# Last sums of a gated feed-forward tile issued behind the next gate job's fifth product; the norms' scales spread by transposes

## The chip, the cores and the metric

The kernel runs on one core of one Trainium2 chip, in one launch. The metric is device microseconds of that core. TensorE (PE in the profile, PEld for its weight loads) multiplies; ScalarE (ACT), VectorE (DVE) and GpSimd (POOL) do the rest, and transfers are issued from the queues of SyncE (SP), ScalarE and GpSimd.

## What is computed

One inference step of a two-layer decoder on 512 prompt tokens and 32 sample tokens, 544 columns in all, with a model width of 1024. Layer 0 mixes by a gated short convolution, layer 1 by retention with four heads. After each mixer comes a feed-forward of hidden width 2816. Every block starts from an RMS norm.

```python
def rmsnorm(x, g):
    y = xf * lax.rsqrt(jnp.mean(xf * xf, axis=-1, keepdims=True) + RMS_EPS)
    return (y * g.astype(jnp.float32)).astype(x.dtype)

def swiglu(x, w_gate, w_up, w_down):
    return (jax.nn.silu(x @ w_gate) * (x @ w_up)) @ w_down

for i in range(DEPTH):
    h = rmsnorm(x, norm_mix[i])
    m = short_conv_mixer(h, ...) if i % 2 == 0 else retention_mixer(h, ...)
    x = x + m
    x = x + swiglu(rmsnorm(x, norm_ffn[i]), ffn_w_gate[i], ffn_w_up[i], ffn_w_down[i])
return rmsnorm(x, final_norm), ...
```

## The kernel before

**Layout.** Activations lie transposed: 128 features on the partitions and 544 tokens along the free dimension, as two halves of 272. Every float32 operand is split into a high and a low part (`split`, L202 on ScalarE and L203 on VectorE), and a product is three matmuls: high by high, high by low, low by high.

**Seven products.** The two projections of a feed-forward, and its down projection for most tiles, are done in blocks of 2 by 2 with seven products in place of eight (`Job`, whose matmuls are all at L386). A product has 12 matmuls with a moving operand of 272 columns in a gate or up job, and 9 in most down jobs. A job makes product 1 in a PSUM bank `a`; then come products 6 (into `a`), 5 (into a third bank `c`, from the pool `mm`), 2 (into a bank `b`) and 7 (into `a`); then, in `end`, product 3 into `c` and product 4 into `a`. `take` reads a bank after each step: the products named `u1`, `u2` and `p5` are copied to SBUF by ScalarE (L445, in `summed`), those named `c11`, `c12` and `u3` are added to the copies by VectorE (L447). Product 3 adds to `c` after `p5`, so its first matmul has to wait for the copy of `p5`.

**Order of jobs.** `run` takes the jobs in a row. For each it issues the weight work of the next job (`prepare`), products 6, 5, 2 and 7 of this job, product 1 of the next, and products 3 and 4 of this one. `weights7` does the weight work: sums of the 2 by 2 blocks on VectorE (L336 to L339), splits (L202 and L203; L315 to L317 for the mixed form) and a transfer that adds weights from DRAM to a low part (L318, issued by GpSimd).

**Hidden tiles.** Each layer has 11 pairs of hidden tiles, m = 0 to 10, each with a gate job and an up job (`gate_up`). The gate job ends with the norm's scale, the silu and the scale again (L782 to L785), the up job with products by the gate (L790 to L794). After the up job, `tail(m)` prepares the operands of the down projection: for m = 0 to 8 differences (L717, L720, L721), two splits, a copy of four blocks on ScalarE (`ht`, L722), a negative copy (`lt`, L723) and a transfer that adds the blocks to `lt` (L724, issued by GpSimd). For m = 3 and 6 the tail runs behind the down jobs of the group of three tiles before (`later`); m = 9 and 10 have a plain split. The down jobs of a group come after the next m's gate and up jobs.

**The norms.** `rms_scale` sums squares over features with matmuls that put the sums on the partitions (L272), takes the power -0.5 (GpSimd, L248) into columns of `rN`, waits a number of steps, and then spreads each column over all partitions with a float32 matmul of the column, broadcast to 128 by 128, and an identity (`spread`, L252). It runs four times: in the convolution, in both feed-forwards and before the retention. Six matmuls cover the 544 tokens, of 128, 128, 16, 112, 128 and 32 columns. The last norm does the same in `scale`, for each half of the tokens, with three matmuls of 128, 128 and 16 columns.

**Order of instructions.** The framework puts each engine's instructions in an order by dependences, a model of durations and the order in which the code issues them. That order is fixed when the program is built. Every engine works through its own in order.

Of the kernel before, what the change touches and what calls it, by code (L numbers as in the profile page):

```python
# [7 lines left out]
F32 = mybir.dt.float32  # L8
F32R = mybir.dt.float32r
AF = mybir.ActivationFunctionType  # L10
ALU = mybir.AluOpType

P = 128
D = 1024
KT = D // P
SEQ = 512
NB = 8
DS = 4
NS = NB * DS
# [4 lines left out]
HT = T // 2  # L24
# [28 lines left out]
def hybrid_decode_kernel(ctx: ExitStack, tc: tile.TileContext, a: dict, o: dict):  # L53
    nc = tc.nc
# [6 lines left out]
    def nm(s):  # L61
        uid[0] += 1
        return f"{s}_{uid[0]}"
# [3 lines left out]
    kinds, at = ["m"], [0]  # L67
# [5 lines left out]
    def psum():  # L73

        kind = kinds[0][at[0] % len(kinds[0])]
        at[0] += 1
        if kind == "s":
            return [bank(), bank()]
        return ps.tile([P, 2, 512], F32, tag="mm", name=nm("mm"), bufs=2)
# [4 lines left out]
    def half(pt, hf):  # L84
        return pt[hf] if isinstance(pt, list) else pt[:, hf, :]

    def each(fn, pt, *aps):

        if isinstance(pt, list):
            for hf in range(2):  # L90
                fn(pt[hf][:, :HT], *[ap[:, hf, :] for ap in aps])
        else:
            fn(pt[:, :, :HT], *aps)
# [5 lines left out]
    mask_p, where_p, rest = cb[:, :512], cb[:, 512:1024], cb[:, 1024:1312]  # L99
    mask_s, ident, mean_w = rest[:, :NS], rest[:, NS : NS + P], rest[:, NS + P :]  # L100
# [33 lines left out]
    rN = resid.tile([P, 6], F32, tag="rN", name="rN")  # L134
# [107 lines left out]
    def rsqrt(out, var, n, eps=None):  # L242

        if eps is None:
            nc.vector.tensor_scalar_add(out, var, EPS)
        else:
            nc.vector.tensor_add(out, var, eps)
        nc.gpsimd.tensor_tensor(out, out, expo[: out.shape[0], :n], op=ALU.pow)  # L248

    def spread(out, tt, lo, hi):  # L250

        return nc.tensor.matmul(  # L252
            out, rN[:, tt : tt + 1].to_broadcast([P, P]), ident[:, lo:hi], start=True, stop=True, skip_group_check=True
        )

    def rms_scale(sample=False, pt=None, rest=4):

        n = 6 if sample else 5  # L260
        pt = pt or psum()
        ms = half(pt, 0)[:, 496:502]
        cols = [slice(tt * P, (tt + 1) * P) for tt in range(4)] + [slice(T - P, T), slice(SEQ, T)]
        for tt in range(n):
            lhs = sqacc[:, cols[tt]]
            if tt == 5:
                lhs = sqlast[:, :P]
                nc.vector.tensor_copy(
                    lhs.rearrange("p (g c) -> p g c", c=NS),
                    sqacc[:, SEQ:].unsqueeze(1).to_broadcast([P, P // NS, NS]),  # L270
                )
            nc.tensor.matmul(ms[:, tt : tt + 1], lhs, mean_w[:, 0:1], start=True, stop=True)  # L272
            if tt < n - 1:
                yield
        rsqrt(rN[:, :n], ms[:, :n], n)
        for _ in range(rest):
            yield

        for tt, hf, at, lo, hi in (
            (0, 0, 0, 0, P), (1, 0, P, 0, P), (2, 0, 2 * P, 0, HT - 2 * P),  # L280
            (2, 1, 0, HT - 2 * P, P), (3, 1, 3 * P - HT, 0, P), (4, 1, SEQ - HT, P - NS, P),
        ):
            spread(half(pt, hf)[:, at : at + hi - lo], tt, lo, hi)
        each(lambda p, r: nc.scalar.activation(r, p, AF.Copy), pt, R)

    def drain(steps):
# [167 lines left out]
    with ExitStack() as c0:  # L454
# [65 lines left out]
        sums = {}  # L520
# [67 lines left out]

        c, b = temp("c"), temp("b")
        nc.gpsimd.memset(u[:, :, NSLOT : NSLOT + 2], 0.0)  # L590
        steps = rms_scale(rest=5)
        pts = [start()]
        for d, pt in zip((b, c), pts[0]):
            each(lambda p, di: nc.scalar.activation(di, p, AF.Copy), pt, halves(d[:, 0, :]))
# [67 lines left out]
        for i, n in enumerate(PAIRED[0]):  # L662
            if i < 2:
                wh, wl, pt = early[i]
                project(pt, wh, wl, 0, yh, yl, first=False, ks=(KT - 2, KT - 1))
            else:
                wh, wl = load_piece(a["cvout"][n], KT * P)
                pt = psum()
# [4 lines left out]
    def ffn(layer, next_gain, then=None):  # L673
        with ExitStack() as c1:
# [19 lines left out]
                s = m % KP  # L694
                return (xh[s], xh[s + KP]), (xl[s], xl[s + KP])

            turned = {}

            def seven(m):

# [8 lines left out]
            def tail(m, g, u):  # L709
                if m >= last[0]:  # L710
                    hs, ls = hidden(m)
                    for i in range(2):
                        split(hs[i], ls[i], u[:, i, :])
                    return
                b, t = [v.rearrange("p a (b c) -> p (a b) c", b=2) for v in (u, g)]
                (h1, h2, ht), (l1, l2, lt) = seven(m)
                nc.vector.tensor_sub(t[:, 0:2, :], b[:, 1::2, :], b[:, 0:2, :])  # L717
                split(h1, l1, b[:, 0:1, :])
                split(h2, l2, b[:, 2:4, :])
                nc.vector.tensor_sub(t[:, 2, :], b[:, 3, :], t[:, 0, :])  # L720
                nc.vector.tensor_sub(t[:, 3, :], b[:, 2, :], t[:, 2, :])  # L721
                nc.scalar.activation(ht, t, AF.Copy)  # L722
                nc.scalar.activation(lt, ht.bitcast(F32), AF.Copy, scale=-1.0)  # L723
                nc.gpsimd.dma_start(lt, t, accum_op=ALU.add)  # L724
                turned[m] = [
                    {1: p[0][:, 0, :], 2: p[1][:, 0, :], 3: p[1][:, 1, :],
                     5: p[2][:, 0, :], 7: p[2][:, 1, :], 6: p[2][:, 2, :], 4: p[2][:, 3, :]}
                    for p in ((h1, h2, ht), (l1, l2, lt))
                ]
# [40 lines left out]
            def gate_up(m):  # L770
                made = {}

                def tile2(tag):
                    if tag not in made:
                        made[tag] = tp.tile([P, 2, T], F32, tag="gu", name=nm(tag))
                    return made[tag]

                def gate(what, src):
                    g = tile2("g")
                    r = R.rearrange("p a b -> p (a b)").unsqueeze(1).to_broadcast([P, 2, T])  # L780
                    if what == "c21":
                        nc.scalar.activation(g[:, 1, :HT], src, AF.Copy)  # L782
                        nc.vector.tensor_mul(g, g, r)
                        nc.scalar.activation(g, g, AF.Silu)
                        nc.vector.tensor_mul(g, g, r)  # L785

                def up(what, src):
                    g, u = tile2("g"), tile2("u")
                    if what == "u3":
                        nc.vector.tensor_mul(u[:, 1, HT:], u[:, 1, HT:], g[:, 1, HT:])  # L790
                    elif what == "c12":
                        nc.vector.tensor_mul(u[:, 0, :], u[:, 0, :], g[:, 0, :])
                    elif what == "c21":
                        nc.vector.tensor_mul(u[:, 1, :HT], src, g[:, 1, :HT])  # L794
                        if m and m % GROUP == 0:

                            later[m] = lambda: tail(m, g, u)
                        else:
                            tail(m, g, u)

                return [
                    Job(
                        [a["ffgu"][layer, 2 * j + q] for j in (m, m + HJ)],
                        lambda k, which: [t[k][:, OPERAND[which], :] for t in (oh, ol)], sw,
                        summed(lambda tag="gu"[q]: tile2(tag), (gate, up)[q]),
                        (lambda: psum()[:, 0, :]) if m else None,
                    )
                    for q in range(2)
                ]
# [67 lines left out]
            steps = rms_scale(rest=9)  # L877
# [10 lines left out]
    def final(ms, acts, group_weights, fp, tp):  # L888
# [4 lines left out]
        sums = {}  # L893
# [21 lines left out]
        def scale(hf):  # L915
            pt = bank()
            mq = pt[:, 496:499]

            of = (sqacc, sqlast)[: hf + 1]
            for t in of:  # L920
                for i, at in enumerate((0, P, HT - P)):
                    cols = slice(hf * HT + at, hf * HT + at + P)
                    last_sum[hf] = nc.tensor.matmul(
                        mq[:, i : i + 1], t[:, cols], mean_w[:, 0:1], start=t is of[0] and (hf == 0 or i == 0),
                        stop=t is of[-1], skip_group_check=True,
                    )
                if t is not of[-1]:
                    yield
            with tc.issue_after(first_product[0].ins) if hf else ExitStack():
                nc.vector.tensor_scalar_add(rN[:, :3], mq, EPS)  # L930
            powers[hf] = nc.gpsimd.tensor_tensor(rN[:, :3], rN[:, :3], expo[:, :3], op=ALU.pow)
            yield
            for i, (lo, hi) in enumerate(((0, P), (0, P), (3 * P - HT, P))):
                last_spread[0] = spread(pt[:, i * P : i * P + hi - lo], i, lo, hi)
            sums[hf] = pt[:, :HT]

        def copied(hf):
# [16 lines left out]
        last_sum, last_spread, powers, first_product, last_store = {}, [None], {}, [None], [None]  # L954
# [18 lines left out]
        rest = scale(1)  # L973
# [796 lines left out]
```

## Time and profile before

| what | value |
|---|---|
| three runs: median (lowest to highest) | 1404.88 us (1404.77 to 1405.04) |
| the profiled execution's own time | 1405.36 us |
| its span, from first to last instruction | 1403.6 us |
| TensorE, busy of the span | 99% |
| VectorE, ScalarE, GpSimd, busy of the span | 81%, 59%, 16% |
| granted TensorE clock, mean | 0.999 |

The profile is of one execution. A line such as `L386 PE MATMUL sm<-oh,wh` is the source line, the engine, the operation, and the tile that is written and those that are read, without buffer numbers. Matmuls overlap: one takes 0.29 us from start to end, while the next starts after 0.12 us. So the distance from start to start tells what a matmul costs, and a busy TensorE may still hold short waits. A float32 matmul that isn't a split product is recorded as two.

### The profile page before, as it was taken

Reading aid. Unit: us, or ns where it says so; the run is one execution under the profiler, and the core shown is the slowest. Engines: PE = TensorE matmul, PEld = TensorE weight load, DVE = VectorE, ACT = ScalarE, POOL = GpSimd, SP = SyncE. Lnnn points to the kernel's source line nnn. Section 1 sums busy time; section 2 is a strip of 40 time slices with the busy share of each in tenths; the row PEclk is TensorE's granted clock in tenths of the full one; section 3 lists DMA queues with packets and bytes.
Section 4 is the critical chain, followed back from the end, with each engine's and each line's share of the span. In section 5 each row is a group of like instructions: output and inputs, shape, how many; then the busy total and the mean of one; then the engine's idle time right before and its main releaser. Section 6 shows DMA issues by size and latency. Waiting matters only on the chain.

```text
span 1403.6 us, 26578 instructions
## 1 busy us (share of the span) xinstructions
PE 1390.2 (99%) x10454; PEld 1317.3 (94%) x10454; DVE 1132.1 (81%) x1923; ACT 822.9 (59%) x1286; POOL 219.4 (16%) x255
## 2 busy tenths in 40 slices
PE   9999999999999999999999999999999999999997
PEld 8999999999999999999967877877899999999997
DVE  6987889898989878676867576586799898989884
ACT  7666567667677657666632313224387767677654
POOL 0111011212221213111200000000111212121212
PEclk9999999999999999999999999999999999999999
DMA  6476346777676754677667355465766777777742
GB/s 206 119 169 166 108 106 159 168 173 183 143 188 151 168 120 134 185 199 201 212 212 240 121 209 184 144 235 181 211 143 153 169 176 172 154 184 153 165 106 87
DMA packets 99295, 233.69 MB, mean 166 GB/s; under 512 B 9793, under 2 KB 33489, under 8 KB 98785
## 3 DMA queue, kind: packets, MB, share of 16 engines
q1 hardware_dynamic: 68032, 167.47, 38.4%
q0 software_dynamic: 28688, 56.61, 23.5%
q10 hardware_dynamic: 2448, 7.91, 1.5%
q8 instruction: 82, 1.34, 0.4%
q14 instruction: 45, 0.36, 0.1%
HBM read 191.84 MB, written 28.42 MB: 157 GB/s over the span
## 4 chain that ended last, share of the span: by engine, by line
PE 93%; DVE 2%; issue 2%; DMA 2%; POOL 0%; ACT 0%; SPq 0%; DVEq 0%; POOLq 0%; ACTq 0%
PE sm L386 43%; PE mm L386 16%; PE mm L187 14%; PE sm L187 4%; PE sm L1262 2%; PE sm L1264 2%; PE sm L1263 2%; PE sm L175 2%; PE sm L177 1%; PE sm L176 1%; PE sm L1483 1%; DVE S L1506 1%; PE mm L1270 1%; DMA wl<-in_rtout_dram 1%; PE mm L1422 0%
## 5 line engine op out<-in xcount | busy, mean ns | idle before, releaser
L386 PE MATMUL sm<-oh,wh 128*128 128x272 f32 x856 | 247.8, 289 | 0.5 <-DVE b L447 0.5
L386 PE MATMUL sm<-ol,wh 128*128 128x272 f32 x856 | 246.1, 288 | 0.0
L386 PE MATMUL sm<-oh,wl 128*128 128x272 f32 x856 | 246.1, 287 | 0.0
L202 ACT ACTIVATE h<-w 128x1024 fp32r<-128x1024 f32 (+3 forms) x170 | 136.5, 804 | 106.3 <-PE mm L386 92.9
L203 DVE TENSOR_TENSOR l<-w,h 128x1024 fp32r<-128x1024 f32 (+3 forms) x170 | 153.6, 904 | 28.1 <-ACT h L202 25.3
L315 ACT ACTIVATE wh<-w 128x1024 fp32r<-128x1024 f32 (+1 forms) x134 | 133.7, 998 | 56.7 <-PE sm L386 48.5
L386 PEld LDWEIGHTS sm<-oh,wh 128*128 128x128 f32 x856 | 161.3, 188 | 2.0 <-DVE b L447 0.9
L386 PEld LDWEIGHTS sm<-oh,wl 128*128 128x128 f32 x856 | 161.1, 188 | 0.0
L386 PEld LDWEIGHTS sm<-ol,wh 128*128 128x128 f32 x856 | 160.8, 188 | 0.1
L386 PE MATMUL sm<-parts,wh 128*128 128x272 f32 x736 | 142.5, 288 | 0.0
L202 ACT ACTIVATE wh<-w 128x1024 fp32r<-128x1024 f32 (+3 forms) x76 | 68.0, 898 | 120.3 <-PE mm L187 62.1
L318 POOL DMA_DIRECT2D wl<-in_ffgu_dram x87 | 81.7, 939 | 328.2 <-ACT wl L317 94.2
L386 PE MATMUL mm<-oh,h 128*128 128x272 f32 x396 | 115.5, 292 | 0.0
L386 PEld LDWEIGHTS sm<-parts,wh 128*128 128x128 f32 x736 | 115.5, 188 | 0.0
L386 PE MATMUL mm<-oh,l 128*128 128x272 f32 x396 | 113.5, 287 | 0.0
L386 PE MATMUL mm<-ol,h 128*128 128x272 f32 x396 | 113.3, 286 | 0.0
L316 DVE TENSOR_TENSOR wl<-w,wh 128x512 fp32r<-128x512 f32 (+1 forms) x134 | 87.2, 651 | 26.4 <-ACT wh L315 26.2
L386 PE MATMUL sm<-parts,wl 128*128 128x272 f32 x368 | 106.2, 289 | 0.3 <-DMA wl<-in_rtqk_dram 0.2
L317 ACT ACTIVATE wl<-wh 128x512 fp32r<-128x512 f32 (+1 forms) x173 | 102.8, 594 | 2.0
L203 DVE TENSOR_TENSOR wl<-w,wh 128x1024 fp32r<-128x1024 f32 (+3 forms) x76 | 79.8, 1055 | 13.1 <-ACT wh L202 12.4
L187 PE MATMUL mm<-parts,wh 128*128 128x272 f32 x488 | 82.4, 290 | 1.4 <-ACT wh L202 1.4
L386 PE MATMUL sm<-oh,h 128*128 128x272 f32 x284 | 82.2, 289 | 0.0
(377 smaller groups left out, 3837.7 us busy)
## 6 DMA issues: line engine op xcount, KB each, us to landing
w<-in_ffgu_dram SPq DMA_DIRECT2D x66, 512.0 KB
wl<-in_ffgu_dram POOLq DMA_DIRECT2D x87, 256.0 KB, 5.2
S<-in_rets_dram SPq DMA_DIRECT2D x16, 1024.0 KB
out_rets_dram<-S SPq DMA_DIRECT2D x16, 1024.0 KB
w<-in_ffdn_dram SPq DMA_DIRECT2D x36, 384.0 KB
cb<-in_ffgu_dram SPq DMA_DIRECT2D x22, 512.0 KB
w<-in_cvin_dram SPq DMA_DIRECT2D x21, 512.0 KB
wl<-in_ffdn_dram POOLq DMA_DIRECT2D x48, 192.0 KB, 4.8
```

The lines of the kernel that those rows point to most:

```text
L175: nc.tensor.matmul(out, lh, rh, start=start, stop=False, skip_group_check=True)
L187: last_product[0] = nc.tensor.matmul(half(pt, hf)[:, :HT], w[:, c], act[k][:, hf * HT : (hf + 1) * HT], start=(first and k == ks[0] and i ...
L202: h = nc.scalar.activation(dh, src, AF.Copy)
L203: last_low[0] = nc.vector.tensor_sub(dl, src, dh.bitcast(F32))
L315: nc.scalar.activation(wh, w, AF.Copy)
L316: last_mixed[0] = nc.vector.tensor_sub(wl[:, :n], w[:, :n], wh[:, :n].bitcast(F32))
L317: nc.scalar.activation(wl[:, n:], wh[:, n:].bitcast(F32), AF.Copy, scale=-1.0)
L318: nc.gpsimd.dma_start(wl[:, n:], src[:, 1, :] if len(src.shape) == 3 else src[:, n:], accum_op=ALU.add)
L386: last = nc.tensor.matmul(out, w[:, c], b, start=(first and j == 0 and i == 0), stop=(j == len(self.ks) - 1 and i == 2), skip_group_check= ...
L1262: nc.tensor.matmul(out, xh[kt][:, ts_], wh[:, cw], start=(kt == 0), stop=False)
L1263: nc.tensor.matmul(out, xh[kt][:, ts_], wl[:, cw], start=False, stop=False)
L1264: last = nc.tensor.matmul(out, xl[kt][:, ts_], wh[:, cw], start=False, stop=(kt == KT - 1))
```

## The change

1. `spread` makes a transpose of the broadcast column, in place of a matmul with the identity, when it has 128 columns. `rms_scale` takes pieces of 128 columns where it can: the third piece of the first half and the last piece of the second are widened, and one of 112 columns stays a matmul. In the convolution's norm nothing changes (`turned=False`). The last norm's third pieces are widened too.
2. In `tail`, the copy `ht`, the negative copy `lt` and the transfer are put on a list. The next gate job issues them when its `p5` has been copied.

```diff
+    def spread(out, tt, lo=0, hi=P, turned=True):
+
+        column = rN[:, tt : tt + 1].to_broadcast([P, P])
+        if turned and hi - lo == P:
+            return nc.tensor.transpose(out, column, ident)
+        return nc.tensor.matmul(out, column, ident[:, lo:hi], start=True, stop=True, skip_group_check=True)
...
-        for tt, hf, at, lo, hi in (
-            (0, 0, 0, 0, P), (1, 0, P, 0, P), (2, 0, 2 * P, 0, HT - 2 * P),
-            (2, 1, 0, HT - 2 * P, P), (3, 1, 3 * P - HT, 0, P), (4, 1, SEQ - HT, P - NS, P),
+        whole = (0, P)
+        for tt, hf, at, (lo, hi) in (
+            (0, 0, 0, whole), (1, 0, P, whole), (2, 0, 2 * P, whole if turned else (0, HT - 2 * P)),
+            (2, 1, 0, (HT - 2 * P, P)), (3, 1, 3 * P - HT, whole),
+            (4, 1, HT - P, whole) if turned else (4, 1, SEQ - HT, (P - NS, P)),
         ):
-            spread(half(pt, hf)[:, at : at + hi - lo], tt, lo, hi)
+            spread(half(pt, hf)[:, at : at + hi - lo], tt, lo, hi, turned)
...
-        steps = rms_scale(rest=5)
+        steps = rms_scale(rest=5, turned=False)
...
-                nc.scalar.activation(ht, t, AF.Copy)
-                nc.scalar.activation(lt, ht.bitcast(F32), AF.Copy, scale=-1.0)
-                nc.gpsimd.dma_start(lt, t, accum_op=ALU.add)
+
+                def sums():
+                    nc.scalar.activation(ht, t, AF.Copy)
+                    nc.scalar.activation(lt, ht.bitcast(F32), AF.Copy, scale=-1.0)
+                    nc.gpsimd.dma_start(lt, t, accum_op=ALU.add)
+
+                waiting.append(sums)
...
-                    if what == "c21":
+                    if what == "p5":
+                        while waiting:
+                            waiting.pop(0)()
+                    elif what == "c21":
...
-            for i, (lo, hi) in enumerate(((0, P), (0, P), (3 * P - HT, P))):
-                last_spread[0] = spread(pt[:, i * P : i * P + hi - lo], i, lo, hi)
+            for i, at in enumerate((0, P, HT - P)):
+                last_spread[0] = spread(pt[:, at : at + P], i)
```

In the built program the two versions differ on each engine as follows. On ScalarE, at 14 places (m = 0, 1, 2, 4, 5, 7, 8 of both layers) the copy of `p5` stands ahead of `ht`; before it stood behind `ht`, a weight copy (L315), `lt` and a second weight copy (L317). For m = 3 and 6 the order is the same as before. At 8 of the 14 (m = 0, 1, 4, 7) the silu (L784) has changed places with a weight split (L202) later in the gate job. On VectorE the additions of `c11` and `u3` (L447) each move ahead of weight work, and at the same 8 places the second scaling of the gate (L785) moves ahead of a weight split (L203); at the first down job of a group some sums change places with additions to `x`. On TensorE, three matmuls of the up job's product 5 stood ahead of the gate job's product 3 at each of the 14 places and now stand behind its product 4; beside that only the spreads differ. The orders on SyncE and on GpSimd are the same.

More of the change, by code (lines that the diff above doesn't have):

```diff
@@ L248, in rsqrt, with rms_scale @@
         nc.gpsimd.tensor_tensor(out, out, expo[: out.shape[0], :n], op=ALU.pow)
[L250 to L256, printed above, removed]
+    def spread(out, tt, lo=0, hi=P, turned=True):
[3 more added lines that the diff above has]
+        return nc.tensor.matmul(out, column, ident[:, lo:hi], start=True, stop=True, skip_group_check=True)
+    def rms_scale(sample=False, pt=None, rest=4, turned=True):
         n = 6 if sample else 5
@@ L695, in hidden @@
                 return (xh[s], xh[s + KP]), (xl[s], xl[s + KP])
-            turned = {}
+            turned, waiting = {}, []
             def seven(m):
```

## The prediction

> **What bounds the kernel.** I read the page first, then TensorE's busy time by stretches, then the order of time around the moved copy.
>
> ```profile
> PE 1390.2 (99%) x10454; PEld 1317.3 (94%) x10454; DVE 1132.1 (81%) x1923; ACT 822.9 (59%) x1286; POOL 219.4 (16%) x255
> PE 93%; DVE 2%; issue 2%; DMA 2%; POOL 0%; ACT 0%; SPq 0%; DVEq 0%; POOLq 0%; ACTq 0%
> ```
>
> TensorE is busy for 99% of the span and holds 93% of the chain that ended last. So what counts is what TensorE has to do and where it is held up. Matmuls overlap, so a short hold-up hides in "busy". It shows in the weight loads (PEld), which run without a gap when nothing holds them:
>
> ```profile
> core 0: us, PE busy (x) PEld busy (x) DVE busy (x) ACT busy (x) POOL busy (x), PEclk, DMA share, GB/s
> 208.00:470.00 262.00, 262.00 (x2090) 261.10 (x2088) 234.57 (x411) 184.13 (x291) 54.77 (x63) 1.00 0.73 165
> 1051.00:1312.00 261.00, 261.00 (x2081) 260.10 (x2081) 233.75 (x410) 184.07 (x291) 54.77 (x63) 1.00 0.74 166
> 269.00:332.00 63.00, 63.00 (x507) 63.00 (x506) 54.99 (x101) 42.06 (x67) 13.69 (x16) 1.00 0.76 175
> ```
>
> The first two stretches hold most of the gate, up and down jobs of the two feed-forwards, with the seven places of each where a moved tail stood; in each the loads miss 0.90 us. The third lies between two of the tails that the change moves, and there they miss nothing. It also gives the price of a matmul: 63 us / 506 = 0.1245 us, call it 0.125. Seven tails of a layer are moved, so 0.90 / 7 = 0.13 us of missing loads would fall to each. The place itself:
>
> ```profile
> 225.87 0.29 PE L386 MATMUL mm<-ol,h 128*128 128x272 f32 x1
> 226.00 0.29 PE L386 MATMUL mm<-oh,l 128*128 128x272 f32 x1
> 226.19 0.40 PE L386 MATMUL mm<-oh,h 128*128 128x272 f32 x1
> 226.42 0.29 PE L386 MATMUL mm<-ol,h 128*128 128x272 f32 x1
> 226.19 0.19 PEld L386 LDWEIGHTS mm<-oh,h 128*128 128x128 f32 x1
> 221.12 0.29 PE L386 MATMUL mm<-oh,l 128*128 128x272 f32 x1
> 221.32 1.06 ACT L202 ACTIVATE h<-w 128x1024 fp32r<-128x1024 f32 x1 [0.26 <-PE mm L386]
> 222.29 1.10 ACT L722 ACTIVATE parts<-g 128x1088 fp32r<-128x1088 f32 x1
> 223.29 1.04 ACT L315 ACTIVATE wh<-w 128x1024 fp32r<-128x1024 f32 x1
> 224.24 1.10 ACT L723 ACTIVATE parts<-parts 128x1088 fp32r<-128x1088 f32 x1
> 225.24 0.61 ACT L317 ACTIVATE wl<-wh 128x512 fp32r<-128x512 f32 x1
> 225.76 0.38 ACT L445 ACTIVATE g<-mm 128x272 f32<-128x272 f32 x1
> ```
>
> Product 5 of the gate job is finished when its last matmul ends, at 221.12 + 0.29 = 221.41. Its copy (L445, `g<-mm`) stands behind `ht` (L722), a weight copy, `lt` (L723) and another weight copy, and ends at 225.76 + 0.38 = 226.14. The first matmul of product 3, at 226.19, comes just after that. Its load starts together with it, where a load usually leads, and it lasts 0.40 us in place of 0.29. From 226.00 to 226.42 two steps take 0.42 us where 2 x 0.125 = 0.25 is the price: 0.17 us lost, of which 0.13 are the missing loads. So ScalarE, idle 41% of the span, holds up TensorE here by its order alone.
>
> **Part 1, the tails.** The copy moves ahead of `ht`, behind the weight split that ends at 221.32 + 1.06 = 222.38. Product 5 is ready by then, so ScalarE doesn't wait for it, and the copy ends near 222.7: 3.4 us sooner, and 3.3 us before product 3, which starts at about 226.0 once the three matmuls ahead of it are behind product 4. The wait goes. Gain: 14 x 0.17 = 2.4 us, between 0 (something else takes its place) and 14 x 0.2 = 2.8 (the rows' rounding).
>
> What is queued behind the copy is 0.38 us later: `ht`, the weight copy, `lt`, the second weight copy, which ends at 226.2. The copies after that keep their times, since `p5` was ahead of them before too. `lt`'s transfer is issued 0.4 us later, on GpSimd, and its order against the weight transfers (L318) is kept, so these are at most 0.4 us later too. The first moved tail whose `lt` is read soon is that of m = 2:
>
> ```profile
> L724 POOL DMA_DIRECT2D f<-g x6: 865/865/893, 267.9 to 1301.1; - x6
> DMA to landing us min/median/max: 6.0/6.8/9.5
> L386 PEld LDWEIGHTS sm<-f,h x48: 187/188/192, 282.0 to 1338.9; 128*128 128x128 f32 x48
> ```
>
> Issued at 267.9 and landed 9.5 us later at the latest, 277.4, or 277.8 when moved. The down jobs read these blocks first at 282.0: 4 us are left. It costs nothing. SyncE's order is the same; its loads wait for weight buffers that come free at most some tenths later.
>
> **Part 2, the spreads.** Four transposes of the retention stand beside the spreads of the second feed-forward's norm:
>
> ```profile
> 1049.24 1.42 PE L252 MATMUL mm<-cb,rN 128*128 128x128 f32 x12
> 1050.50 0.37 PE L386 MATMUL sm<-oh,wh 128*128 128x272 f32 x1
> 741.52 0.60 PE L1422 MATMUL mm<-cb,yn 128*128 128x128 f32 x4
> 741.88 0.48 PE L175 MATMUL sm<-mid,qkhl 128*128 128x512 f32 x1
> 742.20 0.39 PE L176 MATMUL sm<-mid,qkhl 128*128 128x512 f32 x1
> L1422 PE MATMUL mm<-cb,yn x64: 270/273/329, 741.5 to 1003.2; 128*128 128x128 f32 x64
> ```
>
> The six matmuls are recorded as 12: each goes through twice. From 1049.24 to the next matmul are 1.26 us, and that one lasts 0.37 in place of 0.29, so 0.08 more is theirs: 1.34 us, or 0.112 a pass, whatever its width (the 16 and 32 columns are in this mean). The four transposes are recorded once each. To the next matmul are 0.36 us, and that one lasts 0.48 in place of 0.39: 0.45, or 0.11 each. Five transposes and one matmul of two passes make 5 x 0.11 + 2 x 0.112 = 0.77. A norm gains 1.34 - 0.77 = 0.57 us, and three norms (both feed-forwards, retention) gain 1.7. All three stand in a stream of matmuls, so a shorter spread is time of the path. No row shows a transpose of a broadcast column, but the spread reads the same broadcast as its weights now; the bounds are 0 and 1.7.
>
> Weighed against that: the Trainium skill, "TensorE: Matmul & The Clock Gate", section "Part 4: PE-mode transpose", says that a 128 x 128 transpose takes about 275 ns in a kernel and doesn't count as activity for the clock gate. Its figure agrees with the 0.273 us of the row as the time from start to end; as a price in a stream it doesn't, for four would make 1.1 us and the row has 0.60 from the first start to the last end. By it as a price a norm would lose 0.25 us. What it says of the clock no row here shows for so short a run of transposes.
>
> In the last norm three matmuls of two passes become three transposes, 0.67 to 0.33 us, twice:
>
> ```profile
> 1391.64 0.81 PE L923 MATMUL sm<-cb,sqacc 128*128 128x1 f32 x6
> 1391.73 0.43 ACT L234 ACTIVATE sqlast<-x 128x272 f32<-128x272 f32 x1 [0.18 <-DVE x L902]
> 1392.32 0.81 PE L923 MATMUL sm<-cb,sqlast 128*128 128x1 f32 x6
> 1394.38 0.84 PE L252 MATMUL sm<-cb,rN 128*128 128x128 f32 x6
> 1394.30 2.91 POOL L947 TENSOR_TENSOR ya<-ya,R 128x272 f32<-128x272 f32 x4
> ```
>
> After the first spread TensorE sums squares; the last sums (1392.32) need `sqlast`, ready at 1392.16, so at most 0.16 us is to be had. Behind the second spread, a copy and VectorE's products come 0.25 sooner, but GpSimd's four products end at 1397.21 either way and hold ScalarE's last stores. Between 0 and 0.4; I take 0.1.
>
> **Sum.** 2.4 + 1.7 + 0.1 = 4.2 us. The profiled execution took 1405.36 us, 0.48 above the median of the runs: 1401.2 in its own time, 1400.7 as a median.
>
> **Rivals.**
>
> *The wait stays, with another name.* Product 3 or 4 waits for something that was hidden behind the copy. Against it: VectorE's addition of `u3`, which product 4 needs, itself waited for that copy and comes sooner now; stretches without a moved tail miss no loads. For it: VectorE is 81% busy. Only part 2 is left: 1404.9 - 1.8 = 1403.1. Chance 0.10.
>
> *A transpose holds TensorE from start to end.* 5 x 0.273 + 0.22 = 1.59 against 1.34: three norms lose 0.75, the last one some 0.1. 1404.9 - 2.4 + 0.85 = 1403.3. This is also what the skill's figure as a price would make. Against it stands the row of four in 0.60 us. Chance 0.04.
>
> *Transfers take back what layer 0 gains.* Then of the 4.2 the half of the first feed-forward and the retention's norm go, 1.2 + 2 x 0.57 = 2.3: 1403.0. For it: the DMA share of 0.73 in the first stretch. Against it: DMA has 2% of the chain. Chance 0.08.
>
> *Slower: a weight split comes too late.* At 8 of the places (m = 0, 1, 4, 7) the silu (L784) moves ahead of a split of weights (L202), and the second scaling (L785) ahead of its low part (L203).
>
> ```profile
> 231.08 1.28 DVE L783 TENSOR_TENSOR g<-g,R 128x1088 f32<-128x1088 f32 x1
> 232.01 1.06 ACT L202 ACTIVATE h<-w 128x1024 fp32r<-128x1024 f32 x1 [0.49 <-PE mm L386]
> 232.98 1.10 ACT L784 ACTIVATE g<-g 128x1088 f32<-128x1088 f32 x1
> 233.10 1.23 DVE L203 TENSOR_TENSOR l<-w,h 128x1024 fp32r<-128x1024 f32 x1 [0.74 <-ACT h L202]
> 234.25 1.29 DVE L785 TENSOR_TENSOR g<-g,R 128x1088 f32<-128x1088 f32 x1
> 239.42 0.29 PE L386 MATMUL sm<-oh,h 128*128 128x272 f32 x1
> ```
>
> The silu then waits for L783 until 232.36 and ends at 233.46, L785 ends at 234.75, and the low part, ready at 234.33 before, is ready at 234.75 + 1.23 = 235.98, 1.65 us later. Its first reader is at 239.42, so 3.4 us are left. If they were not there and TensorE waited out 1 us at each of the 8 places, the time would be 1400.7 + 8 = 1408.7; it becomes slower from 0.5 us each. Chance 0.06.
>
> **How the numbers follow.** The forecast, 1400.7, has the other 0.72. Its own range, from the bounds of the tails and of the last norm, is 1400.0 to 1402.0. The range for 8 in 10 takes in most of the three rivals near 1403 and half a microsecond below: 1399.5 to 1403.3. About 0.2% (2.8 us) is what can be told from no change, so faster means below 1402.1. Faster: the forecast and a share of the middle rivals that come out smaller, 0.75. Same: 0.18. Slower: 0.07.
>
> **What would show it.** Right: in the stretches of the two feed-forwards the weight loads miss next to nothing; the `mm` matmul after the copy lasts 0.29 us; L722 follows the copy (L445); each norm's spread has seven records in about 0.7 us; `h` and `l` of the swapped places are ready at least 2 us ahead of TensorE. Wrong: loads still missing 0.1 us or more per moved tail, a transpose every 0.27 us, or new waits of TensorE on L203 or L318.

## The result, and the profile after

The changed kernel took 1399.64 us as a median of 7 runs (1399.59 to 1401.45), the kernel before 1404.88 (7 runs, 1404.07 to 1405.40): a ratio of 0.9964, with a 95% interval of 0.9955 to 0.9973. That is 5.2 us, where 4.2 had been forecast. The profiled execution has a span of 1397.8 us against 1403.6.

The page of the kernel after, its first part and the shares of the chain of waits:

```profile
PE 1385.4 (99%) x10433; PEld 1314.1 (94%) x10433; DVE 1131.6 (81%) x1923; ACT 824.0 (59%) x1286; POOL 219.3 (16%) x255
PE 92%; DVE 4%; DMA 1%; issue 1%; ACT 1%; POOL 0%; SPq 0%; DVEq 0%; POOLq 0%; ACTq 0%
```

TensorE bounds the kernel as before. It runs 21 records fewer: three norms save five each (12 to 7), the last one twice three. The same stretches of the two feed-forwards as before, each engine's busy time in them (the lines have moved by 3 to 10 in the code):

```profile
207.00:469.00 262.00, 262.00 (x2100) 262.00 (x2100) 236.27 (x416) 184.93 (x293) 54.78 (x63) 1.00 0.74 167
1046.00:1307.00 261.00, 261.00 (x2094) 261.00 (x2093) 235.45 (x414) 184.87 (x291) 54.76 (x63) 1.00 0.74 167
```

The weight loads (third time of a row) miss nothing, where each stretch had missed 0.90 us. The first moved tail, by ScalarE's and TensorE's order of time:

```profile
220.71 0.38 ACT L448 ACTIVATE g<-mm 128x272 f32<-128x272 f32 x1
220.99 1.10 ACT L727 ACTIVATE parts<-g 128x1088 fp32r<-128x1088 f32 x1
221.99 1.05 ACT L318 ACTIVATE wh<-w 128x1024 fp32r<-128x1024 f32 x1
222.95 1.10 ACT L728 ACTIVATE parts<-parts 128x1088 fp32r<-128x1088 f32 x1
223.94 0.61 ACT L320 ACTIVATE wl<-wh 128x512 fp32r<-128x512 f32 x1
...
224.05 0.28 PE L389 MATMUL sm<-oh,wl 128*128 128x272 f32 x1
224.17 0.29 PE L389 MATMUL mm<-oh,h 128*128 128x272 f32 x1
...
225.66 0.29 PE L389 MATMUL sm<-oh,wh 128*128 128x272 f32 x1
```

The copy (L448) now ends at 221.09, 3.1 us ahead of product 3, whose first matmul starts 0.12 us behind the one before it and lasts 0.29 us. It is the same at every place. Before, at all 14, the first matmul of product 3 started 0.05 us behind the end of the copy and lasted 0.39 or 0.40 us; behind every other copy of an `mm` bank in the gate and up jobs it came at least 1.1 us later and lasted 0.29. After, product 3 of a gate job comes 2.9 us or more behind the copy everywhere, and its first matmul lasts 0.29.

The spread of the second feed-forward's norm and the matmul behind it:

```profile
1045.51 0.49 PE L254 MATMUL mm<-cb,rN 128*128 128x128 f32 x3
1045.84 0.37 PE L255 MATMUL mm<-cb,rN 128*128 128x112 f32 x2
1046.05 0.38 PE L254 MATMUL mm<-cb,rN 128*128 128x128 f32 x2
1046.19 0.37 PE L389 MATMUL sm<-oh,wh 128*128 128x272 f32 x1
```

Seven records in 0.68 us, and a next matmul longer by 0.08: 0.76 in place of 1.34.

To see where all of the 5.77 us between the two spans went, I cut each trace at its spreads: a stage runs from the first matmul behind one spread to the first record of the next, and a spread is its stretch up to the next matmul, with 0.08 added where that one is longer. The values are worked out from TensorE's order of time (in the last rows above, 1045.51 to 1046.27).

| us | before | after | difference |
|---|---|---|---|
| start, to the convolution's spread (code unchanged) | 34.04 | 33.07 | -0.97 |
| to the first feed-forward's spread | 170.17 | 170.22 | +0.05 |
| first feed-forward, 7 tails | 354.29 | 352.86 | -1.43 |
| retention, behind its norm | 486.61 | 486.45 | -0.16 |
| second feed-forward, 7 tails | 340.48 | 339.11 | -1.37 |
| the three spreads | 1.45 + 1.34 + 1.34 | 0.81 + 0.76 + 0.76 | -1.80 |
| from the last norm's first spread to the end | 12.53 | 12.45 | -0.08 |

So the parts that the change touches give 2.80 + 1.80 + 0.08 = 4.7 us, and 1 us more is in stages that it does not touch: the start, the one behind the convolution's norm and the retention. In these three every engine has the same instructions in the same order in both kernels.

### The profile page after: what moved, and what is told of

It reads as the page before. It is cut to its first block, busy times and chain, and to the rows that moved or that the text cites. A ratio compares the mean times of both kernels' runs of the same rounds, so it can differ in the third digit from the quotient of the medians.

```text
span 1397.8 us, 26508 instructions
## 1 busy us (share of the span) xinstructions
PE 1385.4 (99%) x10433; PEld 1314.1 (94%) x10433; DVE 1131.6 (81%) x1923; ACT 824.0 (59%) x1286; POOL 219.3 (16%) x255
## 3 DMA queue, kind: packets, MB, share of 16 engines
q8 instruction: 81, 1.33, 0.4%
## 4 chain that ended last, share of the span: by engine, by line
PE 92%; DVE 4%; DMA 1%; issue 1%; ACT 1%; POOL 0%; SPq 0%; DVEq 0%; POOLq 0%; ACTq 0%
PE sm L389 43%; PE mm L389 16%; PE mm L187 14%; PE sm L187 4%; PE sm L1272 2%; PE sm L1274 2%; PE sm L1273 2%; PE sm L175 2%; PE sm L177 2%; PE sm L176 1%; PE sm L1493 1%; DMA w<-in_cvin_dram 1%; DVE S L1516 1%; PE mm L1280 1%; PE mm L1432 1%
## 5 line engine op out<-in xcount | busy, mean ns | idle before, releaser
L202 ACT ACTIVATE h<-w 128x1024 fp32r<-128x1024 f32 (+3 forms) x170 | 136.4, 803 | 94.6 <-PE mm L389 81.2
L203 DVE TENSOR_TENSOR l<-w,h 128x1024 fp32r<-128x1024 f32 (+3 forms) x170 | 153.6, 904 | 21.4 <-ACT h L202 19.4
L202 ACT ACTIVATE wh<-w 128x1024 fp32r<-128x1024 f32 (+3 forms) x76 | 68.1, 898 | 119.9 <-PE mm L187 61.4
L320 ACT ACTIVATE wl<-wh 128x512 fp32r<-128x512 f32 (+1 forms) x173 | 103.0, 595 | 2.2
L203 DVE TENSOR_TENSOR wl<-w,wh 128x1024 fp32r<-128x1024 f32 (+3 forms) x76 | 80.1, 1057 | 12.4 <-ACT wh L202 11.6
```

Source lines behind the costliest of these rows:

```text
L202: h = nc.scalar.activation(dh, src, AF.Copy)
L203: last_low[0] = nc.vector.tensor_sub(dl, src, dh.bitcast(F32))
L320: nc.scalar.activation(wl[:, n:], wh[:, n:].bitcast(F32), AF.Copy, scale=-1.0)
```

## The experiments

Medians of one group of runs are compared with the kernel before as it ran in that group: 1404.70, 1404.65 and 1404.88 us in the three groups, in which the runs stand in this order.

### Each part alone, and both kernels again

The kernel before and the kernel after, unchanged:

> The kernel before once more, with nothing changed. Theory: of the 5.8 us by which the two profiles' spans differ, 0.94 arises within the first 15 us, where neither version differs from the other, so it is an accident of when the first loads land; this run's ratio to the kernel before is 1.000 (0.9993 to 1.0007), and the first long wait of TensorE in its trace (1.44 us at 7.3 us in the profile of before, 0.46 in that of after) is somewhere else than 1.44, 0.4 to 1.5. Rival: the start belongs to the program, and the wait is 1.4 us again.

> The changed kernel once more. Theory: the two parts add, 4.2 to 4.9 us, and the rest of the 5.2 us between the medians is the accident of the start: ratio 0.9965 to 0.9970, with a first long wait between 0.4 and 1.5 us. Rival (the start belongs to the program): 0.9960 to 0.9963 and a first wait of 0.46 us.

The tails alone: `spread` by matmuls everywhere, as before, and the three lines behind `waiting`:

```diff
-                nc.scalar.activation(ht, t, AF.Copy)
...
+                waiting.append(sums)
...
-    def rms_scale(sample=False, pt=None, rest=4):
+    def rms_scale(sample=False, pt=None, rest=4, turned=False):
...
-                last_spread[0] = spread(pt[:, i * P : i * P + hi - lo], i, lo, hi)
+                last_spread[0] = spread(pt[:, i * P : i * P + hi - lo], i, lo, hi, False)
```

> The moved sums of the tails alone; all spreads are matmuls as before. Theory: 14 waits of 0.17 to 0.20 us go, 2.4 to 2.8 us: ratio 0.9980 to 0.9983, weight loads without a gap in the gate and up jobs, and between two of the places nothing gained. Rival 1 (the gains need each other, or the start belongs to the moved order): 3.5 us or more, 0.9975 or less. Rival 2 (a wait in another place takes some back): under 1.5 us, above 0.9989.

The spreads alone: `spread` and its callers as after, the sums in their old place:

```diff
-                waiting.append(sums)
+                sums()
```

> The spreads by transposes alone; the tails are issued as before. Theory: three norms gain 0.57 each and the last one 0.1 to 0.3, 1.8 to 2.0 us: ratio 0.9986, the 14 waits stay as they were with 0.9 us of missing weight loads in each feed-forward. Rival (the transposes are worth more than their own time, or the start belongs to them): 2.7 us or more, 0.9981 or less. Rival (a transpose holds TensorE for its 0.27 us): 0.6 us slower, 1.0004.

| | median us | ratio, 95% interval | feed-forwards | three spreads | last norm to end |
|---|---|---|---|---|---|
| before again | 1405.44 | 1.0002 [0.9993, 1.0011] | 354.21, 340.50 | 1.44, 1.34, 1.34 | 12.54 |
| tails only | 1402.08 | 0.9979 [0.9971, 0.9988] | 352.83, 339.10 | 1.44, 1.34, 1.34 | 12.53 |
| spreads only | 1402.57 | 0.9984 [0.9975, 0.9992] | 354.22, 340.46 | 0.81, 0.76, 0.76 | 12.44 |
| after again | 1399.12 | 0.9961 [0.9948, 0.9973] | 352.87, 339.11 | 0.81, 0.76, 0.76 | 12.45 |

The stages separate the two parts to a few hundredths: the tails take 1.38 to 1.46 us from each feed-forward and nothing from a spread, the spreads the reverse. By the medians the parts gain 2.6 and 2.1, together 4.7; both at once gained 5.6 here and 5.2 in the first comparison, which the intervals don't tell from 4.7. The ratios alone don't decide either: those of the parts lie just below what the theories expected, that of both is the rival's 0.9960 to 0.9963, and each interval holds the theory's figure and the rival's nearest one. It is the stages that decide. The wait of 1.44 us at 7.3 us, in which the first stage of the kernel before was long, is not in its repeat; there seven matmuls at 4.7 us take 2.14 us together in place of 1.44. So the place of that wait was an accident.

### The sums one copy further back

From the kernel after: `ht`, `lt` and the transfer behind the next up job's first copy.

```diff
-                    if what == "p5":
-                        while waiting:
-                            waiting.pop(0)()
-                    elif what == "c21":
+                    if what == "c21":
...
+                    if what == "u1":
+                        with tc.issue_after(last_copy[0].ins):
+                            while waiting:
+                                waiting.pop(0)()
```

> The kernel after, with ht, lt and lt's transfer put one copy further back: behind the up job's first copy instead of behind the gate job's copy of product 5. lt's transfer is then issued some 3 to 4 us later than in the kernel after. The prediction left 4 us between its landing and its first reader (m = 2). Theory (the sums have slack to spare): 1399.3 us, as the kernel after, within 0.3. Rival (the slack is already used up): the down jobs' first matmuls on lt wait, at one to four places of each feed-forward 1 us or more each, so 1401 to 1407.

Measured 1400.82 us (0.9971 [0.9959, 0.9982]), which is over the 0.3 us allowed. But the feed-forwards took 352.87 and 339.12 us, as after, and TensorE's order is that of the kernel after. GpSimd's transfers of the four last blocks, and their first reader among TensorE's weight loads, first in the kernel after, then here:

```profile
L729 POOL DMA_DIRECT2D f<-g x6: 865/865/891, 266.2 to 1295.9; - x6
DMA to landing us min/median/max: 6.1/6.7/9.6
...
L389 PEld LDWEIGHTS sm<-f,h x48: 187/188/192, 279.8 to 1333.2; 128*128 128x128 f32 x48
```

```profile
L731 POOL DMA_DIRECT2D f<-g x6: 865/865/877, 270.1 to 1299.9; - x6
DMA to landing us min/median/max: 5.4/5.5/5.8
...
L389 PEld LDWEIGHTS sm<-f,h x48: 187/188/192, 280.4 to 1333.9; 128*128 128x128 f32 x48
```

The landing times are of all 18 transfers of the line, not of these six alone, so the longest is an upper bound. After, 279.8 - 266.2 - 9.6 = 4.0 us are left at the latest landing, as the prediction had it. Issued 3.9 us later (3.3 against the first reader, which comes 0.6 later too) the transfers landed in 5.8 us at most, so 4.5 are left. No place waits. In the profiled execution, 0.7 us longer than that of the kernel after, the missing time lies in the first stage, which comes ahead of all this: 33.88 us here against 33.07 (see the repeats below).

### Each transpose twice

```diff
         if turned and hi - lo == P:
+            nc.tensor.transpose(out, column, ident)
             return nc.tensor.transpose(out, column, ident)
```

> The kernel after, with every transpose of the spreads done twice into the same place: 15 more transposes in the three norms that stand in a stream of matmuls, 6 more in the last norm. Theory (0.11 us each in a stream): 15 x 0.11 = 1.65 for the three norms, 0.3 to 0.66 for the last one, so 2.0 to 2.3 over the kernel after: 1401.4, and a norm's spread 1.32 in place of 0.77. Rival (a transpose holds TensorE for the 0.27 us from its start to its end): 21 x 0.27 = 5.7, so 1405.0.

Measured 1401.94 us (0.9979 [0.9969, 0.9988]), and the spreads 1.35, 1.31 and 1.31 us: 0.55 for five more transposes, 0.11 each. TensorE's order of time in the second feed-forward's norm:

```profile
1047.66 0.28 PE L254 MATMUL mm<-cb,rN 128*128 128x128 f32 x1
1047.78 0.27 PE L255 MATMUL mm<-cb,rN 128*128 128x128 f32 x1
1047.89 0.27 PE L254 MATMUL mm<-cb,rN 128*128 128x128 f32 x1
1047.99 0.27 PE L255 MATMUL mm<-cb,rN 128*128 128x128 f32 x1
```

Each lasts 0.27 and the next begins 0.11 behind it: the 0.27 is the time from start to end and not the price. That rival is out. In the last norm six more transposes added only 0.10 us (12.55 against 12.45), less than the 0.3 to 0.66 expected. So these stages give 1.7 us; the rest of the 2.3 between the medians is in none of them.

### One sum left in its old place

From the kernel after, with `ht` ahead of the copy again and `lt` behind it.

```diff
-                def sums():
-                    nc.scalar.activation(ht, t, AF.Copy)
+                nc.scalar.activation(ht, t, AF.Copy)
+
+                def sums():
```

> The kernel after, but ht stays where it was, ahead of the gate job's copy of product 5; lt and its transfer alone stand behind that copy. The copy ends some 2 us later than in the kernel after and 1.5 us earlier than before, so about 1.4 us ahead of product 3. Theory (only a copy later than product 3's turn costs): the whole gain of the tails stays, 1399.3, and the first matmul of product 3 never lasts longer than 0.30. Rival (what stands ahead of the copy costs in proportion): some half of the tails' 2.8 us is lost, 1400.7.

Measured 1399.95 us (0.9965 [0.9953, 0.9978]); feed-forwards 352.86 and 339.13. ScalarE's order at the same place, and the first stretch of this kernel:

```profile
220.31 1.10 ACT L726 ACTIVATE parts<-g 128x1088 fp32r<-128x1088 f32 x1
221.31 1.04 ACT L318 ACTIVATE wh<-w 128x1024 fp32r<-128x1024 f32 x1
222.26 0.38 ACT L448 ACTIVATE g<-mm 128x272 f32<-128x272 f32 x1
```

```profile
207.00:469.00 262.00, 262.00 (x2101) 262.00 (x2100) 236.66 (x417) 185.04 (x293) 54.73 (x63) 1.00 0.73 167
```

The median lies between the two expectations; the stages decide. The copy ends at 222.64, behind two activations, and the loads miss nothing. At all 14 places product 3 starts 1.1 us behind the end of its copy (1.4 had been expected), and its first matmul lasts 0.29 us. The whole gain of the tails stays: a copy that is 1.1 us in time costs no more than one that is 3.1 us in time. So what the kernel before lost was one short wait at each place, not a share of what stood in the queue.

### The other way: `ht` computed twice, in the kernel before

```diff
                 nc.scalar.activation(ht, t, AF.Copy)
+                nc.scalar.activation(ht, t, AF.Copy)
                 nc.scalar.activation(lt, ht.bitcast(F32), AF.Copy, scale=-1.0)
```

> The kernel before, with ht computed twice, so that the copy of product 5 comes one more activation of 1.0 us later. Theory (TensorE waits for that copy at each of 14 places, and has nothing else to do meanwhile): each place loses 1.0 us more than before, 1404.9 + 14 = 1419, TensorE's weight loads then miss about 1.1 us a place. Rival (the 0.2 us at a place is not the copy's, but has another cause): no more than 1 or 2 us over 1404.9.

Measured 1406.86 us (1.0011 [1.0003, 1.0020]), 12 us below what my theory expected, which falls with it. TensorE and ScalarE at the first tail, by order of time:

```profile
225.39 0.29 PE L386 MATMUL mm<-oh,h 128*128 128x272 f32 x1
...
226.64 0.29 PE L386 MATMUL mm<-ol,h 128*128 128x272 f32 x1
226.84 0.39 PE L386 MATMUL mm<-oh,h 128*128 128x272 f32 x1
227.07 0.29 PE L386 MATMUL mm<-ol,h 128*128 128x272 f32 x1
...
226.41 0.38 ACT L445 ACTIVATE g<-mm 128x272 f32<-128x272 f32 x1
```

At this place the copy does come 1.0 us later against the matmuls around it, and product 3 (226.84) still starts right behind its end (226.79). But between the last `sm` matmul and product 3 stand eleven matmuls of another product (225.39 to 226.64), where the kernel before has three (to 226.00 in the prediction's rows). The order of TensorE's instructions is laid down when the kernel is built, by a planner with a model of durations; here it put eight more matmuls ahead, 8 x 0.125 = 1.0 us, just the length of the second `ht`. That it did so because it reckons with the copy's end is my reading. The last tenths of the wait remain: here too the two steps around the restart take 0.20 + 0.23 us in place of 0.25.

That is so at eight of the 14 places (m = 0, 2, 4, 7 of both layers). At the other six (m = 1, 5, 8) the planner put the copy ahead of both `ht`, as the change does, and product 3 comes 3.1 us behind it. For this, TensorE is held up at five other places of each layer, by another copy of ScalarE each time. The copy at m = 1, then one of these new places, behind the up job's first copy:

```profile
243.30 0.38 ACT L445 ACTIVATE g<-mm 128x272 f32<-128x272 f32 x1
...
232.72 0.39 ACT L445 ACTIVATE u<-sm 128x272 f32<-128x272 f32 x1
...
233.16 0.40 PE L386 MATMUL sm<-oh,wh 128*128 128x272 f32 x1
```

The matmul that lasts 0.40 us starts 0.05 us behind the end of the copy, as at each of the 18 restarts in the two feed-forwards of this kernel. So a layer has nine short waits in place of seven. The first stretch's row:

```profile
207.00:469.00 262.00, 262.00 (x2084) 260.67 (x2083) 233.86 (x409) 192.37 (x300) 54.68 (x63) 1.00 0.73 165
```

The loads miss 1.33 us in place of 0.90, and the feed-forwards take 0.62 and 0.65 us more (354.91, 341.13); the other 0.9 us of the median is in neither of them. The rival's figure came true, but not its reason: each of the waits is for a copy. My theory failed because the copy came later at only eight places, and there TensorE had other matmuls to do.

### The convolution's norm by transposes too

The change leaves this one norm as it was. A version with it might have beaten both kernels:

```diff
-        steps = rms_scale(rest=5, turned=False)
+        steps = rms_scale(rest=5)
```

> The kernel after, with the convolution's norm (the first of the kernel, left out by the change) spread by transposes too. Theory (five transposes and one matmul of two passes take 0.77 us in place of 1.34 wherever they stand): its spread falls from 1.34 to about 0.77 us, the kernel gains 0.57 us if TensorE sets the pace there, 1398.9. Rival (the convolution's stage waits for loads, so what TensorE saves is waited out before the next matmul): spread shorter, stage not, 1399.5; as the edit also lets the order of the matmuls around it change, a loss of some tenths is possible.

Measured 1405.73 us (1.0003 [0.9995, 1.0012]): 6 us slower than the kernel after. The spread did fall from 1.34 to 0.76, and the stage behind it grew from 170.2 to 175.0. Here too the planner laid another order, on VectorE, ScalarE, GpSimd and TensorE. TensorE's order of time behind the spread, stretches of this stage, and two short ones from the pause:

```profile
75.17 0.41 PE L389 MATMUL sm<-parts,wh 128*128 128x272 f32 x2
78.60 0.59 PE L389 MATMUL sm<-parts,wl 128*128 128x272 f32 x1 [3.02 <-DMA wl<-in_cvin_dram]
78.99 0.43 PE L389 MATMUL mm<-oh,l 128*128 128x272 f32 x1
79.22 0.43 PE L389 MATMUL mm<-oh,h 128*128 128x272 f32 x1
```

```profile
75.30:78.60 3.30, 0.28 (x3) 0.06 (x2) 3.30 (x5) 2.71 (x8) 0.86 (x1) 0.94 0.64 111
78.60:81.50 2.90, 2.90 (x13) 2.90 (x14) 1.89 (x3) 0.00 (x1) 0.00 (x0) 0.50 0.74 158
...
78.00:78.20 0.20, 0.00 (x0) 0.00 (x0) 0.20 (x2) 0.01 (x1) 0.20 (x1) 1.00 0.09 10
78.20:78.40 0.20, 0.00 (x0) 0.00 (x0) 0.20 (x1) 0.00 (x0) 0.12 (x1) 0.53 0.01 0
```

TensorE comes to a product of the next weights 3.0 us before their low part has landed, and behind that pause it runs at half its clock for 2.9 us. TensorE is not early there; the load is late. The kernel after reaches its product of this form at 75.53, about as soon, and has no wait for the load. GpSimd's transfer of that low part, after, then here:

```profile
68.84 0.86 POOL L321 DMA_DIRECT2D wl<-in_cvin_dram  x1 [1.60 <-PE sm L389]
```

```profile
73.52 0.86 POOL L321 DMA_DIRECT2D wl<-in_cvin_dram  x1 [6.25 <-ACT wl L320]
```

It is issued 4.7 us later, behind a weight copy of ScalarE (L320) that ends at 73.23 in place of 68.55. Neither theory named this; the "some tenths" of the expectation were 4.2 us net in this stage (4.8 lost, 0.58 saved). Most of the other 1.9 us between the medians shows in the profile in the retention (487.9 us against 486.5), where no engine's order differs from the kernel after; why it is longer there stays open.

### The last norm put back, and a third run of each kernel

```diff
-            for i, at in enumerate((0, P, HT - P)):
-                last_spread[0] = spread(pt[:, at : at + P], i)
+            for i, (lo, hi) in enumerate(((0, P), (0, P), (3 * P - HT, P))):
+                last_spread[0] = spread(pt[:, i * P : i * P + hi - lo], i, lo, hi, False)
```

> The kernel after, with the last norm alone spread as before (three matmuls of two passes, twice). Theory: 0.1 us slower than the kernel after, since GpSimd's products and the last stores set the end; the stretch from the first of its spreads to the end, 12.45 us after the change, is 12.5. Rival (TensorE's 0.67 us there is all on the path): 0.7 us slower.

Measured 1399.84 us (0.9961 [0.9948, 0.9973]); from the first of these spreads to the end 12.60 us, 0.15 more than after. GpSimd's last products in the two kernels, after and this one:

```profile
1388.53 2.91 POOL L957 TENSOR_TENSOR ya<-ya,R 128x272 f32<-128x272 f32 x4
```

```profile
1388.96 2.91 POOL L957 TENSOR_TENSOR ya<-ya,R 128x272 f32<-128x272 f32 x4
```

They start 3.15 us behind the first spread (1385.38) after and 3.24 behind it (1385.72) here: of TensorE's 0.67 us only 0.09 to 0.15 is on the path, about what the first theory said. The medians (1399.84 here, 1399.64 after) can't tell so small a difference.

> The kernel before once more, for the scatter of its first stage (until the convolution's spread) and of its retention: 1404.8 us; first stage between 33.0 and 34.2 us if the 1 us by which the profile of the kernel after was shorter there is accident; 33.3 or more each time if it belongs to the program.

> The kernel after once more, for the same: 1399.4 us; first stage between 33.0 and 34.2 us if accident, again 33.0 if it belongs to the program. The five stages between the spreads as in the two profiles of it so far within 0.05 us in both feed-forwards.

Measured 1405.76 us (1.0004 [0.9995, 1.0013]) and 1400.26 us (0.9967 [0.9955, 0.9980]). The feed-forwards took 354.13 and 340.50 before, 352.86 and 339.12 after. The first stage took 33.31 and 32.98 us. With the earlier profiles that makes 34.04, 33.37 and 33.31 before against 33.07, 32.97 and 32.98 after, which by these three alone would belong to the program. Against it stands the kernel with the sums further back, 33.88. The waits of TensorE in the first 33 us, before, after and in that kernel:

```profile
PE mm L187 <- ACT wh L202: 1.4, 2, 1.2
```

```profile
PE mm L187 <- ACT wh L202: 0.2, 1, 0.2
```

```profile
PE mm L187 <- ACT wh L202: 1.1, 2, 0.9
```

The wait differs by about 1 us between them, and kernels with the tails moved have long and short first stages: the tails alone took 34.13. The order of every engine's instructions up to there is the same in all of them, and the unchanged kernel before alone differs by 0.7 us. That points to accident; whether the changed kernel starts earlier by some tenths as a rule stays open.

So it is with all that neither part touches. The start, the stage behind the convolution's norm and the retention together took 690.8, 690.5 and 690.4 us in the three profiles before and 689.7, 688.9 and 689.2 in the three after, though every engine's order in them is the same. With the tails alone they took 691.5, with the spreads alone 689.6. By the medians of this group the change gains 1404.88 - 1400.26 = 4.6 us, as much as the stages that it touches; in the two others it was 5.2 and 5.6. So whether anything beside the two parts, up to 1 us, belongs to the change stays open.

## Why the prediction was right, and where its sizes were off

*What bounds the kernel.* Right. TensorE had two kinds of loss in its stream, both shown by the parts alone.

*The tails, 2.4 us forecast, 2.8 measured.* The mechanism was right: the copy is in time, and product 3 no longer waits. The size was 0.20 us a place, not 0.17. The 0.17 was taken from the two steps around the restart. From the last matmul ahead of product 3 to the first one behind it (thirteen steps) the kernel after takes 225.66 - 224.05 = 1.61 us; before they began at 226.00 and ended with this row:

```profile
227.81 0.29 PE L386 MATMUL sm<-oh,wh 128*128 128x272 f32 x1
```

That is 1.81 us, so 0.03 more is in the eleven steps behind the first two, which the prediction took to run at full pace. Its upper bound, 14 x 0.2 = 2.8, was just reached.

*Nothing takes its place.* Right for all three things that could. VectorE's addition of `u3` and the products behind it never held TensorE: the loads miss nothing. The moved transfer had its 4 us (shown by putting it off by 3.3 us more). The low part that is late behind the silu, and its first reader, in the kernel after:

```profile
232.61 1.22 DVE L203 TENSOR_TENSOR l<-w,h 128x1024 fp32r<-128x1024 f32 x1
237.63 0.29 PE L389 MATMUL sm<-oh,h 128*128 128x272 f32 x1
```

It is ready at 233.83, 3.8 us ahead, where 3.4 were worked out. Nor did transfers take anything back in layer 0: its feed-forward gained 1.43 us, the other 1.37.

*The spreads, 1.7 us forecast, 1.80 measured.* Right to 0.1. Two norms gave 0.58 as the sum said (0.57), the first feed-forward's 0.64; there the second record starts 0.21 us behind the first before and 0.16 after, in place of 0.11, a hold-up that the sum did not have. The price of a transpose, 0.11 us in a stream, holds; 0.27 us as a price is excluded. The 0.112 a pass "whatever its width" is true of the mean alone: in the second feed-forward's norm before, the next pass starts 0.03 us behind the first pass of 16 columns, 0.11 behind its second, and 0.18 behind the pass after that. For the sum only the 1.34 us counted.

*The last norm, 0.1 us forecast, 0.08 measured,* and 0.15 when it alone was put back. Right.

*The rest.* The sum of the measured terms is 4.7 us. The remaining 1.1 of the 5.8 in the two profiles lies in stages whose instructions are the same, the first above all, where the profiled execution before waited 1.2 us longer. The prediction had no term for this, nor for the 0.5 that remains of the 5.2 in the medians, which no trace places.

*The range.* The measured 1399.64 lies 0.14 us above the lower end of the range for 8 in 10, and below what the prediction calls its own range, 1400.0 to 1402.0. That it lies inside owes something to luck, since the repeats of the kernel after had medians of 1399.12 and 1400.26. The upper end, 1402.0, does not come out of the bounds that are named: with the tails at 0 it would be 1400.7 + 2.4 = 1403.1.

*What I had wrong about the kernel,* though the prediction didn't rest on it: that a later copy would cost what it is late by. With `ht` computed twice, the planner laid another order: at eight places TensorE did eight other matmuls meanwhile, at six the copy was not late at all, and the cost was two more short waits a layer.

## What to carry to other kernels

Look for loss in a busy TensorE by the weight loads that miss in a stretch, then at the step where a matmul is longer than its like; price such a place from the last matmul ahead of it to the first one behind the whole product, not by the two steps around the restart. Where a planner lays the order, a longer instruction can cost far less than its length, and an edit that is shorter on paper can cost more than it saves by moving others: compare the engines' orders at every place, not at the first alone, and look for transfers that are now issued later than before. Judge gains of a microsecond by stages cut at marks that both traces have, since stages that no edit touches scatter by as much.

## What the runs showed of the hardware that I had not expected

A pause of TensorE of 3.0 us (the convolution's norm by transposes) was enough to halve its clock, and the clock fell before the pause was over: the last matmul started at 75.29 and ended at 75.58, and the granted clock was 1.00 until 78.20 and 0.53 in the next 0.2 us, so 2.6 us behind that end (2.9 behind that start). It was 0.50 in the 2.9 us behind the pause, with 13 matmuls in which one came every 0.23 us in place of 0.125, some 1.3 us of loss on top of the wait. The Trainium skill, "TensorE: Matmul & The Clock Gate", section "Part 1: The HAM clock gate (the "warmup" mystery)", says that the clock falls to half after an idle window of about 3.4 us; here a pause shorter than that did it.

The 18 transfers that add the blocks to `lt` landed sooner when the sums stood one copy further back: in 5.4 to 5.8 us, with a median of 5.5, in place of 6.1 to 9.6, with a median of 6.7. No run here explains it.
